# Hybrid attention/Hyena step: a free list for weight buffers, earlier splits, two more adaLN chunks on VectorE

## The chip, the cores and the metric

The kernel runs on one core of one Trainium2 chip. The time is the device time of one launch in microseconds (us), the median of the runs; lower is better. One further execution is profiled, and everything said of single instructions is read from that one.

## The reference

Two trunk layers run over 256 latent and 128 context tokens of width 2048. Cut to what matters:

```python
for l in range(2):
    mod_ctx = silu(c_ctx) @ w_ada[l] + b_ada[l]      # adaLN: 2048 -> 3*2048
    mod_lat = silu(c) @ w_ada[l] + b_ada[l]
    ctx, kv = mixer_layer(ctx, mod_ctx, None, None, ...)
    lat, _ = mixer_layer(lat, mod_lat, rope, cache[l], ...)

def mixer_layer(x, mod, ...):
    shift, scale, gate = split(mod, 3)
    h = rmsnorm(x, norm_g) * (1 + scale) + shift
    q, k, v, g_att, hy_in, g_hy = split(h @ w_in)    # hy_in is x0 | x1 | vv
    att = attend(rope(norm(q)), rope(norm(k)), v) * silu(g_att)
    x0, x1, vv = split(short_conv(hy_in))
    z = vv * x1
    y = irfft(rfft(z) * rfft(filter)) + bias * z
    hy = x0 * y * silu(g_hy)
    return x + gate * (concat(att, hy) @ w_out)
```

All is float32. Outputs are the normed trunk of both token groups and the keys and values of the context.

## The kernel before

**Layout.** The 384 tokens stand as columns, a feature block of 128 as partitions; the width 2048 is 16 such tiles. `XM` holds the trunk, later the mixed result. A float32 product is made of three fp32r ones: weights and activations are each split into a high and a low part, and hi·hh, hi·hl and lo·hh are summed. `make_h` writes the normed, modulated input as `hh` and `hl`. `split` makes `hi` of half a weight unit by a copy with a cast on ACT (L151) and `lo` by a subtraction on DVE (L152). Each has SPB = 4 buffers.

**Units.** The work is a list of units of 128x2048 weights, loaded by SP as two half buffers `raw` of 128x1024 from a ring of RAWB = 6, which main weights and adaLN weights share (`load_to`, in the order of the list). Main units are "b" (q, k, v: 12 each layer with 36 tiles of 512 columns), "a" (48 matmuls of 384 columns each; per layer 8 for x0, 16 for x1 and z in turn, 8 attention gates, 8 Hyena gates) and "o" (16 of the output projection, L774 adds gate times result to the residual tile `xo`, which L769 loads on SP). An adaLN chunk of 512 features is four units: 12 chunks a layer. The first eight chunks of layer 0 (scale, shift) are computed at the start, with the k and q units in between as the string START says. The other twelve that layer 0's main steps carry are layer 0's gate and layer 1's scale and shift; the four of layer 1's gate are done in layer 1.

**adaLN, two ways.** A chunk marked P in HOW runs on PE: four matmuls a unit (L199) with the conditioning as the stationary operand, then a copy, four transposes (L210), a reduction. A chunk marked D runs on DVE: eight multiply-adds a unit (L264 the first, L266 the rest) into two accumulators `pa`, and at the end of the chunk the column sum on PE (L282) and two transposes (L290). The DVE operations stand in a queue `vq`; `run_q` issues `u.dq` of them at the end of a main step.

**Order.** The schedule is manual: what the program issues first comes first on its engine. A main step of unit u issues, in order: what is left of u's splits, the first half's split of the next unit (if its loads have been issued), u's matmuls, the second half's split of the next unit, u's evacuation (conversion of a convolution, gate, or residual), background work up to a budget (`run_bg`: attention, filters, Hyena transforms), and `dq` adaLN operations. `plan` puts an adaLN unit between two main units and sets `dq` from the lists R_*, at most LB + 8 operations waiting. SP's loads run RAWB half buffers ahead of the unit in hand, whatever its kind.

**The seam.** The last output unit forms the sum of squares' reciprocal root (`rstd1`, `rstd2`), then layer 1's k units start with `make_h` of tiles 0 to 3, and of the others between the k units. A `make_h` of a tile is one DVE product (L347), two ACT passes with scale and bias (L350), a cast into `hh` (L352) and a DVE subtraction into `hl` (L354, L358).

Of the kernel before, what the change touches and what calls it, by code (L numbers as in the profile page):

```python
# [66 lines left out]
def step_kernel(ctx, tc, xT, vec, cst, delta, zfeat, fw, ada, wb, wc, wo, ck, cv, qk1, yT, nk, nv):  # L67
# [3 lines left out]
    rawp = pool("rawp", RAWB)  # L71
# [54 lines left out]
    state = {"load": 0, "step": 0, "dq": 0}  # L126

    class Unit:
        def __init__(self, src, kind, **kw):
            self.src, self.kind, self.kw = src, kind, kw  # L130
            self.raw, self.nxt, self.dq = [None, None], None, 0
            self.mid = False
            self.hi, self.lo = [None, None], [None, None]

    def load_to(n):
        while state["load"] < min(n, 2 * len(units)):
            i, h = divmod(state["load"], 2)
            u = units[i]
            u.raw[h] = rawp.tile([128, 1024], F32, name="raw", tag="raw")
            nc.sync.dma_start(out=u.raw[h], in_=u.src[:, h * 1024:(h + 1) * 1024])  # L140
# [3 lines left out]

    def split(u, h):
        if u is None or u.kind == "ada" or u.hi[h] is not None:
            return
        hi = hip.tile([128, 1024], F32R, name="hi", tag="hi")
# [4 lines left out]
        u.hi[h], u.lo[h] = hi, lo  # L153

# [38 lines left out]
    def ada_mm(u):  # L193
# [4 lines left out]
        for t in range(4):  # L198
            mm(part[32 * t:32 * t + 32, :], scT[:, kc * 4 + t, :], u.raw[t // 2][:, (t % 2) * 512:(t % 2 + 1) * 512],  # L199
               start=(kc == 0), stop=(kc == 3))  # L200
        if kc == 3:
# [38 lines left out]
    pacc = {}  # L240


    vq = []

    def ada_acc(u):
# [5 lines left out]
        def done():  # L251
            st["left"] -= 1
            if st["left"] == 0:
                urgent.append((state["step"] + 1, lambda: ada_sum(l, ch, st)))

        def op(t, v):
            if v not in st:
                st[v] = accs_p.tile([128, 512], F32, name=f"pa{v}", tag=f"pa{v}")
# [8 lines left out]
            done()  # L267
# [5 lines left out]
    def run_q(q, n):  # L273
        for _ in range(n):
# [66 lines left out]
    def make_h(l, kts):  # L341
        ts = []
        for kt in kts:
# [3 lines left out]
            nc.vector.tensor_tensor(t[:, :T], XM[:, kt, :], r[:, :T], ALU.mult)  # L347
        for kt, t in zip(kts, ts):
            for a, b, v in SEG:
                nc.scalar.activation(t[:, a:b], t[:, a:b], AF.Identity, bias=mod[l][:, kt, v:v + 1],  # L350
                                     scale=asc[l][:, kt, v:v + 1])
            nc.scalar.copy(hh[:, kt, :], t[:, :T])  # L352
        for kt, t in zip(kts, ts):
            nc.vector.tensor_tensor(hl[:, kt, :], t[:, :T], hh[:, kt, :].bitcast(F32), ALU.subtract)  # L354
# [437 lines left out]
    def ada_units(l, ch, n=0, how="P"):  # L792
# [276 lines left out]
```

## Time and profile before

| what | value |
|---|---|
| time before, median of 3 runs | 1563.02 us (1561.33 to 1567.05) |
| the profiled execution's own time, and its span | 1566.88 us, 1565.1 us |
| TensorE clock granted, mean | 0.982 |
| busy: PE, PEld, DVE, ACT, POOL | 1500.5, 1302.5, 951.8, 598.8, 22.4 us |
| instructions on PE, DVE, ACT | 8046, 1522, 991 |
| moved by DMA | 286.48 MB, mean 183 GB/s |

PE is busy for 96% of the span, DVE for 61%. The run is cut below at ends of main units on PE:

| stretch of the run, us | main units |
|---|---|
| 0 to 170.0 | start: adaLN of layer 0 with most of its k and q units |
| 170.0 to 195.0 | the last two of those k and q units |
| 195.0 to 283.5 | second half of q, then v, layer 0 (4 + 4 units) |
| 283.5 to 704.0 | x0, x1 and z, gates but the last, layer 0 (39) |
| 704.0 to 861.4 | last gate and output projection, layer 0 (17) |
| 861.4 to 914.3 | the seam and k, layer 1 (4) |
| 914.3 to 949.3 | first half of q, layer 1 (4) |
| 949.3 to 1019.5 | second half of q, then v, layer 1 (4 + 4) |
| 1019.5 to 1401.5 | x0, x1 and z, gates but the last, layer 1 (39) |
| 1401.5 to 1546.6 | last gate and output projection, layer 1 (17) |
| 1546.6 to 1565.1 | final norm and store |

Of adaLN work the start has eight chunks on PE. The stretch from 195.0 to 861.4 has six on PE and six on DVE, layer 1 four on DVE. A row of a view of stretches gives its start and end, its length, then the busy time and the number of instructions of PE, PEld (weight loads of TensorE), DVE, ACT and POOL, the granted clock, the share of the 16 DMA engines that was busy, and GB/s. A view restricted to one line leaves out the engines that the line does not use. A row of single instructions begins with start and length; a bracket gives the wait ahead of the first and what ended it. A row of waits ends with total, count and longest; a row of a group, after the bar, with busy time, mean in ns, then the idle time ahead of its instructions and what ended most of it.

### The profile page before, as it was taken

How to read it: one execution, taken by the hardware profiler on the slowest of the kernel's cores; microseconds unless marked ns; L12 is line 12 of the kernel's file. 1: busy time of each engine (PE TensorE's matmuls, PEld its weight loads, DVE VectorE, ACT ScalarE, POOL GpSimd, SP SyncE). 2: the span in 40 equal slices, each digit the busy share in tenths (PEclk: the TensorE clock that was granted, in tenths of full speed). 3: DMA queues.
4: the chain of work that ended last, by engine and by line, in shares of the span. 5: the costliest groups of instructions: out<-in, count | busy, mean ns of one | idle time of the engine just before them, and what ended most of it. 6: DMA issues, size and time to landing. Idle time of an engine off the chain costs nothing.

```text
span 1565.1 us, 20551 instructions
## 1 busy us (share of the span) xinstructions
PE 1500.5 (96%) x8046; PEld 1302.5 (83%) x8046; DVE 951.8 (61%) x1522; ACT 598.8 (38%) x991; POOL 22.4 (1%) x45
## 2 busy tenths in 40 slices
PE   9998989999999999998899899999999999999996
PEld 5355667878998888998899578899999999999995
DVE  5743466655576666577767464675677767675444
ACT  2433444445433233224323554455543332234331
POOL 1100000000000000000000000000000000000000
PEclk9999999999999999999999899999999999999998
DMA  9867745645566575354677134343345354464432
GB/s 352 340 242 269 268 149 180 208 162 175 179 211 234 184 235 194 138 201 156 220 241 237 65 124 139 135 155 132 124 155 208 103 182 141 165 204 151 154 126 81
DMA packets 81770, 286.48 MB, mean 183 GB/s; under 512 B 9638, under 2 KB 14056, under 8 KB 81160
## 3 DMA queue, kind: packets, MB, share of 16 engines
q1 hardware_dynamic: 78872, 276.63, 51.2%
q0 software_dynamic: 2800, 8.53, 1.4%
q8 instruction: 63, 1.03, 0.3%
q14 instruction: 35, 0.29, 0.1%
HBM read 271.49 MB, written 13.63 MB: 182 GB/s over the span
## 4 chain that ended last, share of the span: by engine, by line
PE 78%; DMA 10%; DVE 6%; ACT 5%; issue 1%; SPq 0%; DVEq 0%; ACTq 0%
PE acc L726 17%; PE acc L728 17%; PE acc L727 17%; DMA raw<-in_wc 6%; PE acc L702 5%; PE acc L701 5%; PE acc L703 5%; PE adab L199 3%; DVE lo L152 2%; ACT hi L151 2%; DMA raw<-in_wb 2%; PE bgb L423 1%; ACT tt L350 1%; PE bgb L563 1%; DVE hl L358 1%
## 5 line engine op out<-in xcount | busy, mean ns | idle before, releaser
L726 PE MATMUL acc<-hh,hi 128*128 128x384 f32 x1792 | 613.5, 342 | 5.5 <-ACT hi L151 4.2
L728 PE MATMUL acc<-hh,lo 128*128 128x384 f32 x1792 | 604.6, 337 | 11.1 <-DVE lo L152 11.1
L727 PE MATMUL acc<-hl,hi 128*128 128x384 f32 x1792 | 603.3, 337 | 1.2 <-DVE hl L358 1.0
L152 DVE TENSOR_TENSOR lo<-raw,hi 128x1024 fp32r<-128x1024 f32 x288 | 344.5, 1222 | 232.6 <-ACT hi L151 230.6
L151 ACT CAST hi<-raw 128x1024 fp32r<-128x1024 f32 x288 | 295.4, 1047 | 342.6 <-DMA raw<-in_wc 253.9
L726 PEld LDWEIGHTS acc<-hh,hi 128*128 128x128 f32 x1792 | 337.5, 188 | 29.0 <-issue 8.9
L728 PEld LDWEIGHTS acc<-hh,lo 128*128 128x128 f32 x1792 | 337.4, 188 | 15.1 <-DVE lo L152 15.0
L727 PEld LDWEIGHTS acc<-hl,hi 128*128 128x128 f32 x1792 | 337.4, 188 | 5.0 <-DVE hl L358 2.3
L266 DVE SCALAR_TENSOR_TENSOR pa<-raw,scT,pa 128x512 f32<-128x512 f32 x300 | 206.4, 746 | 0.0
L701 PE MATMUL acc<-hi,hh 128*128 128x512 f32 x384 | 160.5, 418 | 13.0 <-ACT hh L352 8.8
L702 PE MATMUL acc<-lo,hh 128*128 128x512 f32 x384 | 157.2, 409 | 4.2 <-DVE lo L152 4.2
L703 PE MATMUL acc<-hi,hl 128*128 128x512 f32 x384 | 157.1, 409 | 0.0
L701 PEld LDWEIGHTS acc<-hi,hh 128*128 128x128 f32 x384 | 75.0, 195 | 41.4 <-ACT hh L352 14.1
L702 PEld LDWEIGHTS acc<-lo,hh 128*128 128x128 f32 x384 | 75.1, 195 | 23.7 <-DVE lo L152 6.8
L309 ACT ACTIVATE tt<-XM 128x384 f32<-128x384 f32 x48 | 24.8, 524 | 175.9 <-DVE XM L774 171.6
L703 PEld LDWEIGHTS acc<-hi,hl 128*128 128x128 f32 x384 | 74.9, 195 | 20.5 <-DVE hl L354 2.7
L774 DVE SCALAR_TENSOR_TENSOR XM<-acc,mod,xo 128x256 f32<-128x256 f32 x64 | 23.8, 413 | 87.3 <-PE acc L728 62.5
L199 PE MATMUL adab<-raw,scT 128*32 128x512 f32 x448 | 63.5, 610 | 5.1 <-DMA raw<-in_ada 5.0
L350 ACT ACTIVATE tt<-tt,mod,asc 128x256 f32<-128x256 f32 x64 | 31.5, 540 | 36.4 <-DVE tt L347 36.3
L354 DVE TENSOR_TENSOR hl<-tt,hh 128x384 fp32r<-128x384 f32 x32 | 17.9, 559 | 40.8 <-ACT hh L352 40.8
L199 PEld LDWEIGHTS adab<-raw,scT 128*32 128x32 f32 x448 | 10.4, 108 | 36.7 <-issue 24.5
L620 DVE SCALAR_TENSOR_TENSOR z<-acc,V,z 128x255 f32<-128x255 f32 (+1 forms) x64 | 25.1, 414 | 20.8 <-ACT z L616 19.7
(159 smaller groups left out, 1066.3 us busy)
## 6 DMA issues: line engine op xcount, KB each, us to landing
raw<-in_ada SPq DMA_DIRECT2D x192, 512.0 KB, 4.9
raw<-in_wc SPq DMA_DIRECT2D x160, 512.0 KB, 4.8
raw<-in_wb SPq DMA_DIRECT2D x64, 512.0 KB, 5.3
raw<-in_wo SPq DMA_DIRECT2D x64, 512.0 KB, 5.3
P<-Hd SPq DMA_DIRECT2D x4, 1536.0 KB, 9.2
XM<-in_xT SPq DMA_DIRECT2D x4, 768.0 KB, 9.1
Hd<-P POOLq DMA_DIRECT2D x12, 256.0 KB, 6.1
Hd<-P SPq DMA_DIRECT2D x12, 256.0 KB, 6.6
```

What stands on the lines that cost most here:

```text
L151: nc.scalar.copy(hi, src)
L152: nc.vector.tensor_tensor(lo, src, hi.bitcast(F32), ALU.subtract)
L199: mm(part[32 * t:32 * t + 32, :], scT[:, kc * 4 + t, :], u.raw[t // 2][:, (t % 2) * 512:(t % 2 + 1) * 512], start=(kc == 0), stop=(kc == 3))
L266: nc.vector.scalar_tensor_tensor(out=acc, in0=w, scalar=sc, in1=acc, op0=ALU.mult, op1=ALU.add)
L350: nc.scalar.activation(t[:, a:b], t[:, a:b], AF.Identity, bias=mod[l][:, kt, v:v + 1], scale=asc[l][:, kt, v:v + 1])
L620: nc.vector.scalar_tensor_tensor(out=out[:, o:o + n], in0=bank[:, i:i + n], scalar=w(k), in1=out[:, o:o + n], op0=ALU.mult, op1=ALU.add)
L701: mm(accs[g][m], hh[:, kt, ms], wh[:, k, :], start=first, stop=False)
L702: mm(accs[g][m], hh[:, kt, ms], wl[:, k, :], start=False, stop=False)
L703: mm(accs[g][m], hl[:, kt, ms], wh[:, k, :], start=False, stop=last)
L726: mm(b[:, :T], wh, hh[:, kt, :], start=(kt == 0), stop=False)
L727: mm(b[:, :T], wh, hl[:, kt, :], start=False, stop=False)
L728: mm(b[:, :T], wl, hh[:, kt, :], start=False, stop=(kt == 15))
```

## The change

The ring of half buffers becomes eight named tiles in a free list. `fetch` takes one and issues its load; `release` gives it back at the point of the program where its last reader is issued: for main weights behind the split, for adaLN on PE behind the unit's matmuls, for adaLN on DVE behind the last operation on that half. `load_main` loads main weights as long as buffers are free and at most MAINB = 4 are held by main weights; `load_ada` loads an adaLN unit if two are free and at most ADAB = 4 are held. `plan` is gone: adaLN units are taken from `todo` by `load_ada` at the end of a step.

A step now also splits the first half of the unit after the next, between its evacuation and the background work, so that attention and Hyena work stands behind that split. The order of a step is: matmuls, second half's split of the next unit, loads, evacuation, first half's split of the unit after the next, loads, background work, up to PPS = 2 adaLN units on PE, `dq` adaLN operations, adaLN loads. SPB is 3 for 4.

HOW marks four of the twelve chunks of layer 0 for PE, eight for DVE (before six and six); the four in layer 1 stay on DVE. The lists R_* are new, with R_1 for layer 1. Column sums of finished chunks go through a queue `sums`, which is emptied before the accumulators are reused.

`make_h` is rewritten: per tile two DVE operations (latent and context columns) that apply reciprocal root and scale, two ACT passes that add the bias and write `hh` directly, two DVE operations that form `hl`. A tile had one DVE product, three ACT operations and one DVE subtraction.

```diff
-RAWB = 6
-SPB = 4
+RAWB = 8
+SPB = 3
-HOW = 'PPDDPDPDPDPDDDDD'
+HOW = 'PPDDDDPPDDDDDDDD'
-LB = 2
+MAINB, ADAB, PPS = 4, 4, 2
-R_O = [5] * 15 + [0]
+R_O = [4] + [6] * 14 + [5]
...
+    def fetch(u, h, of=None):
+        u.raw[h], u.of = free.pop(0), of
+        if of:
+            held[of] += 1
+        nc.sync.dma_start(out=u.raw[h], in_=u.src[:, h * 1024:(h + 1) * 1024])
+
+    def release(u, h):
+        free.append(u.raw[h])
+        if u.of:
+            held[u.of] -= 1
...
+    def load_main():
+        load_start()
+        if state["load"] == 2 * len(units):
+            while free and held["main"] < MAINB and state["main"] < 2 * len(mains):
+                i, h = divmod(state["main"], 2)
+                fetch(mains[i], h, "main")
+                state["main"] += 1
+
+    def load_ada():
+        while todo and len(free) >= 2 and held["ada"] <= ADAB - 2:
+            u = todo.pop(0)
+            for h in range(2):
+                fetch(u, h, "ada")
+            if u.kw["how"] == "P":
+                by_pe.append(u)
+            else:
+                ada_acc(u)
...
     def make_h(l, kts):
...
-            nc.vector.tensor_tensor(t[:, :T], XM[:, kt, :], r[:, :T], ALU.mult)
+            for a, b, v in SEG:
+                nc.vector.scalar_tensor_tensor(out=t[:, a:b], in0=XM[:, kt, a:b], scalar=asc[l][:, kt, v:v + 1],
+                                               in1=r[:, a:b], op0=ALU.mult, op1=ALU.mult)
         for kt, t in zip(kts, ts):
             for a, b, v in SEG:
-                nc.scalar.activation(t[:, a:b], t[:, a:b], AF.Identity, bias=mod[l][:, kt, v:v + 1],
-                                     scale=asc[l][:, kt, v:v + 1])
-            nc.scalar.copy(hh[:, kt, :], t[:, :T])
+                nc.scalar.activation(hh[:, kt, a:b], t[:, a:b], AF.Identity, bias=mod[l][:, kt, v:v + 1])
         for kt, t in zip(kts, ts):
-            nc.vector.tensor_tensor(hl[:, kt, :], t[:, :T], hh[:, kt, :].bitcast(F32), ALU.subtract)
+            for a, b, v in SEG:
+                nc.vector.scalar_tensor_tensor(out=hl[:, kt, a:b], in0=t[:, a:b], scalar=mod[l][:, kt, v:v + 1],
+                                               in1=hh[:, kt, a:b].bitcast(F32), op0=ALU.add, op1=ALU.subtract)
...
             {"b": b_evac, "a": a_evac, "o": o_evac}[u.kind](u)
...
-            run_bg(EB if startup else 2.5)
+            if startup:
+                run_bg(EB)
+                continue
+            if u.nxt is not None:
+                split(u.nxt.nxt, 0)
+            load_main()
+            run_bg(2.5)
+            for a in by_pe[:PPS]:
+                ada_mm(by_pe.pop(0))
             run_q(vq, u.dq)
+            load_ada()
```

The rows below are the program's order on one engine. Names are the program's: `raw` or `raw_1xx` a half buffer, `pa` an adaLN accumulator, `xo` a residual tile, `lo` the low part of a weight half, `x2` two alike in a row.

SP's loads in the output projection of layer 0, about two steps of before:

```order
L140 DMA raw<-in_ada 128x1024 x2
L769 DMA xo<-in_xT 128x384
L140 DMA raw<-in_wo 128x1024 x2
L769 DMA xo<-in_xT 128x384
L140 DMA raw<-in_wo 128x1024 x2
```

and of the changed kernel, from one residual load to three later:

```order
L141 DMA raw_105<-in_ada 128x1024
L141 DMA raw_103<-in_ada 128x1024
L817 DMA xo<-in_xT 128x384
L141 DMA raw_107<-in_wo 128x1024
L141 DMA raw_108<-in_wo 128x1024
L141 DMA raw_109<-in_ada 128x1024
L141 DMA raw_104<-in_ada 128x1024
L817 DMA xo<-in_xT 128x384
L141 DMA raw_110<-in_wo 128x1024
L141 DMA raw_106<-in_wo 128x1024
L817 DMA xo<-in_xT 128x384
```

Before, an adaLN unit's loads stood ahead of every second residual load; now they stand ahead of three in four.

DVE in an output unit of layer 0, from one residual sum (two pieces, L774, later L822) to the next, before:

```order
L774 SCALAR_TENSOR_TENSOR XM<-acc,mod_97,xo 128x256
L774 SCALAR_TENSOR_TENSOR XM<-acc,mod_97,xo 128x128
L313 TENSOR_TENSOR acc_93<-acc_93,tt 128x384
L266 SCALAR_TENSOR_TENSOR pa_5527<-raw,scT,pa_5527 128x512
L266 SCALAR_TENSOR_TENSOR pa_5525<-raw,scT,pa_5525 128x512
L266 SCALAR_TENSOR_TENSOR pa_5527<-raw,scT,pa_5527 128x512
L152 TENSOR_TENSOR lo<-raw,hi 128x1024 x2
L774 SCALAR_TENSOR_TENSOR XM<-acc,mod_97,xo 128x256
```

and in the changed kernel:

```order
L822 SCALAR_TENSOR_TENSOR XM<-acc,mod_94,xo 128x256
L822 SCALAR_TENSOR_TENSOR XM<-acc,mod_94,xo 128x128
L359 TENSOR_TENSOR acc_90<-acc_90,tt 128x384
L185 TENSOR_TENSOR lo<-raw_108,hi 128x1024
L312 SCALAR_TENSOR_TENSOR pa_5558<-raw_103,scT,pa_5558 128x512
L312 SCALAR_TENSOR_TENSOR pa_5560<-raw_103,scT,pa_5560 128x512
L312 SCALAR_TENSOR_TENSOR pa_5558<-raw_109,scT,pa_5558 128x512
L312 SCALAR_TENSOR_TENSOR pa_5560<-raw_109,scT,pa_5560 128x512
L312 SCALAR_TENSOR_TENSOR pa_5558<-raw_109,scT,pa_5558 128x512
L312 SCALAR_TENSOR_TENSOR pa_5560<-raw_109,scT,pa_5560 128x512
L185 TENSOR_TENSOR lo<-raw_110,hi 128x1024
L822 SCALAR_TENSOR_TENSOR XM<-acc,mod_94,xo 128x256
```

One of the two lo moved ahead of the adaLN operations, of which there are six instead of three to five. In this step the second operation is the last on half buffer raw_103.

DVE in a step with attention work, between the conversion of a convolution and the next one, before (L532 and L535 are the softmax):

```order
L532 TENSOR_REDUCE mx<-bgb 128x1
L535 RECIPROCAL z<-z 128x1
L532 TENSOR_REDUCE mx<-bgb 128x1
L535 RECIPROCAL z<-z 128x1
L266 SCALAR_TENSOR_TENSOR pa_2409<-raw,scT,pa_2409 128x512
L266 SCALAR_TENSOR_TENSOR pa_2407<-raw,scT,pa_2407 128x512
L266 SCALAR_TENSOR_TENSOR pa_2409<-raw,scT,pa_2409 128x512
L152 TENSOR_TENSOR lo<-raw,hi 128x1024 x2
```

and in the changed kernel (L580 and L583 are the softmax):

```order
L185 TENSOR_TENSOR lo<-raw_104,hi 128x1024
L580 TENSOR_REDUCE mx<-bgb 128x1
L583 RECIPROCAL z<-z 128x1
L580 TENSOR_REDUCE mx<-bgb 128x1
L583 RECIPROCAL z<-z 128x1
L312 SCALAR_TENSOR_TENSOR pa_2137<-raw_109,scT,pa_2137 128x512
L312 SCALAR_TENSOR_TENSOR pa_2139<-raw_109,scT,pa_2139 128x512
L312 SCALAR_TENSOR_TENSOR pa_2137<-raw_109,scT,pa_2137 128x512
L312 SCALAR_TENSOR_TENSOR pa_2139<-raw_109,scT,pa_2139 128x512
L312 SCALAR_TENSOR_TENSOR pa_2137<-raw_103,scT,pa_2137 128x512
L312 SCALAR_TENSOR_TENSOR pa_2139<-raw_103,scT,pa_2139 128x512
L185 TENSOR_TENSOR lo<-raw_107,hi 128x1024
```

One lo moved ahead of the softmax, and six adaLN operations stand where three stood. At the seam the order on DVE behind the reciprocal root is now a lo, five adaLN operations, then the first `make_h`; before it was that `make_h` at once.

More of the change, by code (lines that the diff above doesn't have):

```diff
@@ L125, in step_kernel @@
     units = []
-    state = {"load": 0, "step": 0, "dq": 0}
+    state = {"load": 0, "step": 0, "main": 0}
+    held = {"main": 0, "ada": 0}
+    free = [one.tile([128, 1024], F32, name=f"raw{n}") for n in range(RAWB)]
     class Unit:
@@ L131, in __init__, with load_start @@
             self.raw, self.nxt, self.dq = [None, None], None, 0
-            self.mid = False
+            self.mid, self.of = False, None
             self.hi, self.lo = [None, None], [None, None]
-    def load_to(n):
-        while state["load"] < min(n, 2 * len(units)):
+    def fetch(u, h, of=None):
[7 more added lines that the diff above has]
+            held[u.of] -= 1
+    def load_start():
+        while state["load"] < 2 * len(units) and free:
             i, h = divmod(state["load"], 2)
-            u = units[i]
-            u.raw[h] = rawp.tile([128, 1024], F32, name="raw", tag="raw")
-            nc.sync.dma_start(out=u.raw[h], in_=u.src[:, h * 1024:(h + 1) * 1024])
+            fetch(units[i], h)
             if h == 1 and 4 <= i < 8:
@@ L153, in split @@
         u.hi[h], u.lo[h] = hi, lo
+        release(u, h)
     bg = []
@@ L200, in ada_mm @@
                start=(kc == 0), stop=(kc == 3))
+        for h in range(2):
+            release(u, h)
         if kc == 3:
@@ L238, in have_rstd, with run_sums @@
             ready(j)
-    pacc = {}
-    vq = []
+    pacc, sums = {}, []
+    def run_sums():
+        while sums:
+            sums.pop(0)()
+    vq, by_pe = [], []
     def ada_acc(u):
@@ L249, in ada_acc, with done @@
         st = pacc[0]
-        def done():
+        left = [4, 4]
+        def done(h):
             st["left"] -= 1
+            left[h] -= 1
+            if left[h] == 0:
+                release(u, h)
             if st["left"] == 0:
-                urgent.append((state["step"] + 1, lambda: ada_sum(l, ch, st)))
+                sums.append(lambda: ada_sum(l, ch, st))
+                urgent.append((state["step"] + 1, run_sums))
         def op(t, v):
             if v not in st:
+                run_sums()
                 st[v] = accs_p.tile([128, 512], F32, name=f"pa{v}", tag=f"pa{v}")
@@ L273, in run_q @@
     def run_q(q, n):
-        for _ in range(n):
+        for _ in range(min(n, len(q))):
             q.pop(0)()
@@ L860, in start @@
         nc.sync.dma_start(out=V, in_=vec)
-        load_to(2)
+        for h in range(2):
+            fetch(units[0], h)
+        state["load"] = 2
         nc.scalar.activation(scT[:, :, 0:2], V[:, V_C:V_C + 32].rearrange("p (k v) -> p k v", v=2), AF.Silu)
@@ L951, in step_kernel @@
             split(u, 1)
-            near = u.nxt is not None and u.nxt.raw[1] is not None
+            near = u.nxt is not None and (not startup or u.nxt.raw[1] is not None)
             if near:
```

63 lines of the change are left out of this document (25 added, 38 removed).

## The prediction

> **What bounds it now.** I read the stretches of the run first, then the waits, then single steps. The two layers do the same matrix work, so I cut both at the same units of it. The rows give length, busy time (and instructions) of PE, PEld, DVE, ACT and POOL, the granted clock, the DMA share and GB/s:
>
> ```profile
> 0.00:170.00 170.00, 159.33 (x689) 82.35 (x690) 81.18 (x143) 61.20 (x100) 8.85 (x20) 0.97 0.81 300
> 195.00:283.50 88.50, 81.03 (x362) 60.89 (x361) 53.78 (x87) 37.98 (x78) 1.63 (x3) 0.96 0.50 172
> 949.30:1019.50 70.20, 70.20 (x318) 56.75 (x317) 42.42 (x66) 34.59 (x65) 1.09 (x2) 1.00 0.40 135
> 283.50:704.00 420.50, 412.28 (x2392) 372.88 (x2390) 262.77 (x428) 151.72 (x247) 0.54 (x1) 1.00 0.56 192
> 1019.50:1401.50 382.00, 382.00 (x2208) 367.96 (x2207) 263.00 (x417) 146.69 (x238) 0.54 (x1) 1.00 0.45 155
> 704.00:861.40 157.40, 147.99 (x846) 143.41 (x845) 110.37 (x167) 52.27 (x73) 8.14 (x15) 0.99 0.64 213
> 1401.50:1546.60 145.10, 143.49 (x827) 141.61 (x827) 68.47 (x101) 47.63 (x68) 0.00 (x0) 1.00 0.38 129
> 861.40:914.30 52.90, 44.05 (x161) 30.38 (x160) 27.86 (x46) 33.23 (x61) 1.08 (x2) 0.87 0.20 68
> 1430.00:1513.00 83.00, 83.00 (x480) 83.00 (x480) 36.66 (x50) 25.67 (x32) 0.00 (x0) 1.00 0.46 155
> ```
>
> They are: start; second half of q with v, layer 0 and 1; x0 up to the last gate unit, 0 and 1; that gate unit with the output projection, 0 and 1; the seam between the layers; ten dense output units. The last row gives the yardstick: 480 matmuls in 83.0 us, 8.3 us for a unit of 48. TensorE bounds layer 1. Layer 0 is longer by 18.3, 38.5 and 12.3 us. Part of that is adaLN work on PE, the rest is stalls:
>
> ```profile
> PE acc L728 <- DVE lo L152: 10.5, 11, 3.3
> ACT hi L151 <- DMA raw<-in_wc: 205.2, 66, 9.3
> SPq L140 <- DVE pa L266: 195.0, 48, 10.6
> 283.50:704.00 420.50, 21.31 (x160) 3.15 (x160) 1.00 0.56 192
> L210 PE MATMUL bgb<-C,tt 128*128 128x128 f32 x56 | 9.3, 291 | 0.7 <-ACT tt L203 0.7
> L282 PE MATMUL bgb<-pa,ones 128*32 128x256 f32 x80 | 6.9, 391 | 1.0 <-DVE pa L266 1.0
> L290 PE MATMUL bgb<-C,tt 128*128 128x128 f32 x20 | 4.1, 289 | 0.5 <-ACT tt L284 0.5
> ```
>
> The first three are waits between 170 and 870 us, with total, count and longest; the fourth is L199 alone, adaLN on PE: 160 records, 20 units, 1.07 us each. The chain reads backwards: PE waits for lo, lo for hi, hi for a weight load, and SP holds that load because the ring's next buffer is still read by an adaLN step on DVE.
>
> By the Trainium skill, Perfetto Trace Analysis, "Identifying the Most-Contended Engine", matmul busy time misjudges headroom and LDWEIGHTS busy time is the measure. The trace agrees: in the long stretch PE shows 8.2 us idle, PEld 47.6; by the first alone the stalls there would be capped near 8 us and the sum would come out some 5 us later.
>
> **Fewer chunks on PE.** Two chunks go to DVE. Each gives back 4 units of 1.07 us and its transposes (14 chunks share the 9.3 us of L210, 0.66 each), 4.9 us; each adds column sums (10 chunks share 6.9 + 4.1), 1.1 us. In all −7.6 us of PE. By place: the long stretch keeps 8 of its 20 PE units, the one before it gets 8 instead of 4. On DVE two chunks are 64 operations, priced next.
>
> **Splits earlier.** In an attention step DVE now does, in order, the conversion of a convolution, lo of the second unit ahead, the softmax, six adaLN operations, and the other lo. Rows of before (start, length; then ACT's first pass of a convolution, four steps of layer 1, the cast of a weight half):
>
> ```profile
> 364.36 1.64 DVE L620 SCALAR_TENSOR_TENSOR XM<-acc,V,XM 128x255 f32<-128x255 f32 x4
> 365.92 0.55 DVE L532 TENSOR_REDUCE mx<-bgb 128x1 f32<-128x384 f32 x1
> 368.69 2.06 DVE L266 SCALAR_TENSOR_TENSOR pa<-raw,scT,pa 128x512 f32<-128x512 f32 x3
> 741.02 3.40 DVE L266 SCALAR_TENSOR_TENSOR pa<-raw,scT,pa 128x512 f32<-128x512 f32 x5
> 744.34 2.35 DVE L152 TENSOR_TENSOR lo<-raw,hi 128x1024 fp32r<-128x1024 f32 x2
> L616 ACT ACTIVATE XM<-acc,V 128x384 f32<-128x384 f32 x16 | 10.7, 670 | 27.7 <-PE acc L728 27.7
> 1047.80:1094.10 46.30, 46.30 (x257) 43.37 (x257) 28.64 (x52) 24.87 (x48) 0.00 (x0) 1.00 0.39 128
> L151 ACT CAST hi<-raw 128x1024 fp32r<-128x1024 f32 x288 | 295.4, 1047 | 342.6 <-DMA raw<-in_wc 253.9
> ```
>
> Convolution 1.56 (to the next start), softmax 2.77 (365.92 to 368.69, its waits for ACT inside), an adaLN operation 0.66 apart (five in 3.40, from 741.02 to the lo at 744.34), a lo 1.14 apart (two in 2.35). With 0.75 for ACT's pass ahead (0.67 and the way) that is 0.75 + 1.56 + 1.14 + 2.77 + 6 × 0.66 + 1.14 = 11.3 us. The four steps of layer 1 take PE 46.3, 11.6 each: DVE just fits. It may also run late: lo of the second half is first wanted half a unit, 4.1 us, into the next unit but one. So the x0 and x1 steps should not stall on lo. Nor on loads:
>
> ```profile
> raw<-in_wc SPq DMA_DIRECT2D x160, 512.0 KB, 4.8
> P<-Hd SPq DMA_DIRECT2D x4, 1536.0 KB, 9.2
> ```
>
> With four main half buffers of its own account, a half is fetched when the half two units ahead of it has been split, some 16 us before it is wanted; it lands in 4.8 and may well wait behind an adaLN load on SP. The filter spectra, the other transfer on SP here, are issued two steps ahead of their use and land in 9.2. The long stretch becomes 382.0 + 8 × 1.07 + 1.3 + 1.1 + 1 left = 394, **−26** us (−13 if the stalls stay, −28 if all go).
>
> The stretch before it gets those 4.9 us of PE work. Its stalls, 88.5 − 70.2 − 4.9 = about 13, could fall by as much, since its first two steps no longer have adaLN operations, or stay, since an extra lo now stands ahead of the q/k norms. I take a fall by the same 4.9, in all **0** (−8 to +5).
>
> **Output projection of layer 0.** Here the change hurts. Its residual load xo stands on SP behind the adaLN loads, and these now wait for operations of the step before. What that does is already in the profile, on a light step of before with three adaLN operations:
>
> ```profile
> 778.56 2.07 DVE L266 SCALAR_TENSOR_TENSOR pa<-raw,scT,pa 128x512 f32<-128x512 f32 x3
> 781.04 0.42 SPq L769 DMA_DIRECT2D xo<-in_xT  x1
> 786.72 0.48 DVE L774 SCALAR_TENSOR_TENSOR XM<-acc,mod,xo 128x256 f32<-128x256 f32 x1 [3.82 <-DMA xo<-in_xT]
> DMA to landing us min/median/max: 4.2/5.1/6.5
> 1463.82 0.74 DVE L774 SCALAR_TENSOR_TENSOR XM<-acc,mod,xo 128x256 f32<-128x256 f32 x2 [3.67 <-PE acc L728]
> 1466.10 2.36 DVE L152 TENSOR_TENSOR lo<-raw,hi 128x1024 fp32r<-128x1024 f32 x2 [0.38 <-ACT hi L151]
> ```
>
> The adaLN operations end at 780.63, xo is issued 0.41 later, and DVE stands idle 3.82 us for it. From 755 us on xo lands 5.1 us after issue (4.2 to 6.5): 5.5 from the release. Before, only every second xo follows such a load and the lighter steps make it up. Afterwards nearly every one does. A step is then XM to lo 2.28 (the two 146x rows), lo 1.14, six operations 3.96, lo 1.14: 8.5 us. Between the operation that frees the load and the next XM stand, by the order's rows, 3.8 us (after the second operation), 2.5 (fourth), 1.1 (sixth), or 5.1 (none), in turn. So four steps take 4 × 8.5 − 12.5 + 4 × 5.5 = 43.5 us on DVE against PE's 33.8 with one column sum. Over 15 steps that is 36 us, less 3 for the first, which is still on time: 33 over the 145.1 that layer 1 needs, so 178 or 179 for 157.4, **+22** us. Landings of 4.2 and 6.5 move it by 15 times the difference: +8 and +43.
>
> A rule speaks the other way. By the Trainium skill, DMA: Bandwidth & Descriptors, "Latency and other measured facts", a DMA's fixed cost is about 2 us. With that, plus 0.4, only the 1.1 case would wait and this term would be near −10; the trace's 4.2 to 6.5 for 192 KB disagrees, so the sum goes by the trace.
>
> **Seam.** After rstd DVE now does a lo, which waits for ACT's copy and cast, and five adaLN operations before the first make_h:
>
> ```profile
> 864.96 0.56 DVE L329 TENSOR_TENSOR tt<-C,r 128x384 f32<-128x384 f32 x1
> 867.32 0.48 ACT L338 COPY acc<-bgb 128x384 f32<-128x384 f32 x1 [2.61 <-PE bgb L337]
> 867.90 0.55 DVE L347 TENSOR_TENSOR tt<-XM,bgb 128x384 f32<-128x384 f32 x1
> 869.49 0.51 ACT L352 CAST hh<-tt 128x384 fp32r<-128x384 f32 x1
> 878.86 1.02 DVE L347 TENSOR_TENSOR tt<-XM,acc 128x384 f32<-128x384 f32 x2
> 884.54 1.02 DVE L347 TENSOR_TENSOR tt<-XM,acc 128x384 f32<-128x384 f32 x2
> ```
>
> ACT's copy ends at 867.80. A cast of a weight half, 1.05, + 1.14 for lo + 5 × 0.66 puts the first make_h at 873.3, 5.4 us after 867.90. PE and its clock (0.87 in this stretch) wait with it. But a round of two make_h tiles took 5.68 us (878.86 to 884.54), with DVE waiting for ACT; the change takes one cast of 0.51 a tile off ACT, and DVE's two extra operations a tile run while it would wait. Five rounds of 4.7 give back 5. I take **0** (−4 to +5).
>
> **Start.** Loads run one unit further ahead, eight half buffers for six:
>
> ```profile
> PE adab L199 <- DMA raw<-in_ada: 5.0, 4, 2.2
> ```
>
> PE waits 5.0 us for adaLN loads, all here, and the mean clock of 0.97 over 170 us costs as much again. A unit more, 1.05 MB, is 3.5 us at this stretch's 300 GB/s, more than the longest wait; I take half of both, **−5** (−10 to +1). The smaller hi/lo pool, 3 for 4, delays a second half until half a unit has been used, covered by the 4.1 us above. Layer 1 and the tail: **0**, PE has no stall to lose there.
>
> **Sum.** −5 + 0 − 26 + 22 + 0 = −9. The profiled run has span 1565.1 and took 1566.88, 3.9 above the median of 1563.02; the difference goes on the median. That is 1554.
>
> **Rivals.** (1) *xo is hidden*: the landing shortens as the queue ahead of it empties. Then the output units take about 147, −10 for +22, and the total is 1522. For it: DVE never waited for xo in layer 1. Against: there no adaLN load stands ahead of it. Chance 0.17. (2) *The head start does nothing*: DVE, at 11.3 of 11.6 us, falls behind and the long stretch keeps its 13 us; 1567. For it: the narrow fit; against: the 4.1 us of slack. 0.13. (3) *Slower*: the output projection's xo lands late. It decides from a mean landing of about 6.3 us, where 15 × 1.2 = 18 us more come on top; at 6.5 it gives 1575. For it: 6.5 in the range and more loads on the queue; against: the median of 5.1. 0.15. (4) *The forecast*, 1542 to 1563: 0.55.
>
> Below 0.5% a measurement of this kernel can hardly be told from no change. Of the forecast 0.30 lies under 1555, 0.23 within the bound, 0.02 above. Rival 1 is all faster, rival 2 mostly same (0.02, 0.10, 0.01), rival 3 mostly slower (0, 0.02, 0.13). Faster 0.49, same 0.35, slower 0.16. The range, 1523 to 1575, reaches to the ends of rivals 1 and 3 and leaves a tenth at each side.
>
> **What would show it.** Right: the stretch from x0 to the last gate near 394 us; DVE XM waiting for xo some 3 us in most output units of layer 0, that stretch near 178; the waits of SP for adaLN operations gone from the x0 steps' main loads; PE's idle time before the first k unit of layer 1 up by 5 us. Wrong: xo waits of under 1 us, or lo waits on PE in the x0 steps.

## The result

The changed kernel takes 1601.87 us (median of 4 runs, 1599.10 to 1605.41) against 1562.17 us for the kernel before (4 runs): the ratio is 1.0251, 95% interval 1.0219 to 1.0284. It is slower by about 40 us, where the prediction had 9 us faster; the time lies outside the range of 1523 to 1575.

### The profile page after: what moved, and what is told of

It reads as the page before. It is cut to its first block, busy times and chain, and to the rows that moved or that the text cites. A ratio compares the mean times of both kernels' runs of the same rounds, so it can differ in the third digit from the quotient of the medians.

```text
span 1597.3 us, 20568 instructions
## 1 busy us (share of the span) xinstructions
PE 1495.8 (94%) x7994; PEld 1311.6 (82%) x7994; DVE 1007.2 (63%) x1650; ACT 577.6 (36%) x959; POOL 22.4 (1%) x45
## 4 chain that ended last, share of the span: by engine, by line
PE 45%; DVE 4%; DMA 2%; ACT 1%; issue 1%; SPq 0%; DVEq 0%; ACTq 0%
PE acc L774 11%; PE acc L775 11%; PE acc L776 11%; PE acc L749 3%; PE acc L750 2%; PE acc L751 2%; DVE pa L312 2%; DMA xo<-in_xT 2%; DVE lo L185 1%; ACT hi L184 1%; PE bgb L611 1%; PE bgb L594 1%; PE bgb L328 1%; DVE XM L833 1%; PE bgb L702 0%
## 5 line engine op out<-in xcount | busy, mean ns | idle before, releaser
L774 PE MATMUL acc<-hh,hi 128*128 128x384 f32 x1792 | 617.9, 345 | 0.9 <-ACT hi L184 0.9
L185 DVE TENSOR_TENSOR lo<-raw,hi 128x1024 fp32r<-128x1024 f32 x288 | 351.2, 1221 | 249.2 <-ACT hi L184 248.0
L184 ACT CAST hi<-raw 128x1024 fp32r<-128x1024 f32 x288 | 299.5, 1044 | 325.5 <-PE acc L775 216.0
L774 PEld LDWEIGHTS acc<-hh,hi 128*128 128x128 f32 x1792 | 340.2, 190 | 18.2 <-issue 11.8
L312 DVE SCALAR_TENSOR_TENSOR pa<-raw,scT,pa 128x512 f32<-128x512 f32 x360 | 246.6, 744 | 0.0
L822 DVE SCALAR_TENSOR_TENSOR XM<-acc,mod,xo 128x256 f32<-128x256 f32 x64 | 23.8, 413 | 67.4 <-PE acc L776 37.9
L328 PE MATMUL bgb<-pa,ones 128*32 128x256 f32 x96 | 16.6, 531 | 46.9 <-DVE pa L312 46.9
L233 PE MATMUL adab<-raw,scT 128*32 128x512 f32 x384 | 54.0, 604 | 3.2 <-DMA raw<-in_ada 3.2
L328 PEld LDWEIGHTS bgb<-pa,ones 128*32 128x32 f32 x96 | 3.8, 126 | 54.4 <-DVE pa L312 27.2
L668 DVE SCALAR_TENSOR_TENSOR z<-acc,V,z 128x255 f32<-128x255 f32 (+1 forms) x64 | 25.2, 414 | 31.4 <-ACT z L664 30.2
L668 DVE SCALAR_TENSOR_TENSOR XM<-acc,V,XM 128x255 f32<-128x255 f32 (+1 forms) x64 | 25.2, 414 | 24.6 <-ACT XM L664 23.5
## 6 DMA issues: line engine op xcount, KB each, us to landing
XM<-in_xT SPq DMA_DIRECT2D x4, 768.0 KB, 11.6
```

The lines of the kernel that those rows point to most:

```text
L184: nc.scalar.copy(hi, src)
L185: nc.vector.tensor_tensor(lo, src, hi.bitcast(F32), ALU.subtract)
L312: nc.vector.scalar_tensor_tensor(out=acc, in0=w, scalar=sc, in1=acc, op0=ALU.mult, op1=ALU.add)
L328: mm(b[o:o + 32, 0:256], ones[:, 0:32], acc[v][:, h * 256:(h + 1) * 256], start=True, stop=True)
L668: nc.vector.scalar_tensor_tensor(out=out[:, o:o + n], in0=bank[:, i:i + n], scalar=w(k), in1=out[:, o:o + n], op0=ALU.mult, op1=ALU.add)
L774: mm(b[:, :T], wh, hh[:, kt, :], start=(kt == 0), stop=False)
```

## The profile after

The profiled execution took 1599.1 us, its span is 1597.3 us. It is cut at the ends of the same main units as before: the start with the last k and q units, second half of q with v, x0 up to the last gate, that gate with the output projection, the seam with k, and layer 1 from q on. The columns are those of the stretches before.

```profile
0.00:185.90 185.90, 176.23 (x774) 97.94 (x774) 100.88 (x197) 66.18 (x112) 8.86 (x20) 0.96 0.85 318
185.90:276.00 90.10, 84.85 (x402) 61.91 (x401) 54.19 (x90) 41.35 (x82) 1.64 (x3) 0.98 0.64 218
276.00:694.90 418.90, 401.92 (x2299) 374.62 (x2298) 297.24 (x478) 148.20 (x242) 0.54 (x1) 0.98 0.51 177
694.90:877.50 182.60, 154.45 (x848) 146.57 (x847) 122.56 (x189) 49.55 (x71) 8.12 (x15) 0.93 0.57 193
877.50:935.60 58.10, 40.56 (x161) 31.63 (x160) 42.16 (x89) 23.69 (x47) 1.08 (x2) 0.79 0.33 114
935.60:1579.40 643.80, 634.95 (x3505) 597.05 (x3504) 380.15 (x588) 247.38 (x403) 2.18 (x4) 0.99 0.40 138
```

| stretch | before | after | predicted difference | measured |
|---|---|---|---|---|
| start, last k and q | 195.0 | 185.9 | −5 | −9.1 |
| second half of q, v | 88.5 | 90.1 | 0 | +1.6 |
| x0 to the last gate, layer 0 | 420.5 | 418.9 | −26 | −1.6 |
| output projection, layer 0 | 157.4 | 182.6 | +22 | +25.2 |
| seam and k | 52.9 | 58.1 | 0 | +5.2 |
| layer 1 from q on (before: 914.3 to 1546.6) | 632.3 | 643.8 | 0 | +11.5 |

With 0.6 less in the tail the measured column sums to the spans' difference, 32.2 us. The long stretch kept PE's idle time: 418.90 − 401.92 = 17.0 us, against 8.2 before; 15.0 of the 17.0 are now spent in front of column sums. In layer 1, where almost nothing was to change, 11.5 us are new.

One group of the page, the column sums of the DVE chunks, and three waits of the whole run (total, count, longest):

```profile
L328 PE MATMUL bgb<-pa,ones 128*32 128x256 f32 x96 | 16.6, 531 | 46.9 <-DVE pa L312 46.9
```

```profile
PE bgb L328 <- DVE pa L312: 46.9, 9, 11.5
DVE XM L822 <- DMA xo<-in_xT: 29.4, 12, 5.3
PE acc L776 <- DVE lo L185: 4.1, 7, 0.7
```

The column sum was the harmless row of the profile before: 1.0 us of idle time ahead of it in the whole run. Now PE stands 46.9 us in front of it. The waits for lo, which the change was expected to remove, did fall, from 11.1 us on the page of before to 4.1.

One such wait, in an attention step of layer 1, on PE and then on DVE (start, length, count at the end, idle time ahead and its releaser in brackets):

```profile
1123.27 0.62 PE L328 MATMUL bgb<-pa,ones 128*32 128x256 f32 x4
1127.10 1.07 PE L328 MATMUL bgb<-pa,ones 128*32 128x256 f32 x4 [3.20 <-DVE pa L312]
1128.10 0.69 PE L774 MATMUL acc<-hh,hi 128*128 128x384 f32 x1
```

```profile
1120.84 1.64 DVE L668 SCALAR_TENSOR_TENSOR XM<-acc,V,XM 128x255 f32<-128x255 f32 x4 [2.25 <-ACT XM L664]
1122.40 1.22 DVE L185 TENSOR_TENSOR lo<-raw,hi 128x1024 fp32r<-128x1024 f32 x1
1123.53 0.55 DVE L580 TENSOR_REDUCE mx<-bgb 128x1 f32<-128x384 f32 x1
...
1126.23 0.16 DVE L583 RECIPROCAL z<-z 128x1 f32<-128x1 f32 x1 [0.79 <-ACT P L582]
1126.31 0.73 DVE L312 SCALAR_TENSOR_TENSOR pa<-raw,scT,pa 128x512 f32<-128x512 f32 x1
1126.96 0.48 DVE L310 TENSOR_SCALAR pa<-raw,scT 128x512 f32<-128x512 f32 x1
```

At this step the `vq` queue holds the last operation of one chunk (the L312 at 1126.31) and the first ones of the next (L310). In front of the next chunk's first operation the program calls `run_sums`, so the column sum is issued in the same step, behind this step's matmuls on PE. PE has nothing left ahead of it and stands until DVE has done the evacuation, a lo, the softmax and the last adaLN operation; the matmuls of the next unit, whose operands are ready, stand behind the sum. Before, `plan` never let a step mix two chunks, and the sum came a whole step later. By the Trainium skill, PSUM — Partial Sum Buffer, section "Engine vs sequencer instructions", matmuls start and complete in program order; the trace agrees: no matmul of L774 starts ahead of the sum that waits until 1127.10.

The output projection is late in the main for the reason that the prediction gave: DVE waits 27.6 us for xo there. PE also stands 23.1 us in front of three column sums in this stretch, which the prediction did not have. DVE, from one residual sum to the next but one:

```profile
715.33 0.74 DVE L822 SCALAR_TENSOR_TENSOR XM<-acc,mod,xo 128x256 f32<-128x256 f32 x2 [2.61 <-DMA xo<-in_xT]
...
723.05 0.74 DVE L822 SCALAR_TENSOR_TENSOR XM<-acc,mod,xo 128x256 f32<-128x256 f32 x2 [0.44 <-DMA xo<-in_xT]
724.38 0.56 DVE L359 TENSOR_TENSOR acc<-acc,tt 128x384 f32<-128x384 f32 x1 [0.59 <-ACT tt L355]
725.31 1.23 DVE L185 TENSOR_TENSOR lo<-raw,hi 128x1024 fp32r<-128x1024 f32 x1 [0.38 <-ACT hi L184]
726.46 1.41 DVE L312 SCALAR_TENSOR_TENSOR pa<-raw,scT,pa 128x512 f32<-128x512 f32 x2
728.37 0.49 DVE L310 TENSOR_SCALAR pa<-raw,scT 128x512 f32<-128x512 f32 x1 [0.51 <-PE bgb L328]
```

DVE waits for xo in 11 of these units, and here too a chunk ends in the step (L312, then L310 behind the sum). At the seam, on DVE:

```profile
885.85 0.74 DVE L822 SCALAR_TENSOR_TENSOR XM<-acc,mod,xo 128x256 f32<-128x256 f32 x2 [1.87 <-DMA xo<-in_xT]
...
893.86 1.23 DVE L185 TENSOR_TENSOR lo<-raw,hi 128x1024 fp32r<-128x1024 f32 x1 [3.26 <-ACT hi L184]
895.00 3.40 DVE L312 SCALAR_TENSOR_TENSOR pa<-raw,scT,pa 128x512 f32<-128x512 f32 x5
898.31 0.73 DVE L394 SCALAR_TENSOR_TENSOR tt<-XM,asc,bgb 128x256 f32<-128x256 f32 x2
```

The last residual sum starts at 885.85, 8.4 us after PE finished the last output unit at 877.5: the lag that DVE has gathered is paid here. ACT's copy of the root ended at 892.88, and the first make_h starts 5.4 us later, as priced.

## The experiments

Times are medians, ratios those to the kernel before on the same chip, with the 95% interval; the kernel before took 1562.2 to 1563.3 us in each set of runs, so medians of different sets are compared directly. Three theories stood at first: **S**, the column sum issued in its own step; **X**, the late residual load; and against S, **D**, that DVE has no slack in those steps and PE would only wait elsewhere.

### Chunk and column sum kept a step apart

The entries of the queue carry a mark, `q[0][0]`, for a chunk's first operations.

```diff
     def run_q(q, n):
-        for _ in range(min(n, len(q))):
-            q.pop(0)()
+        more = min(state["carry"], 2) if n else 0
+        n, state["carry"] = n + more, state["carry"] - more
+        while n and q:
+            if q[0][0] and sums:
+                state["carry"] += n
+                break
+            n -= 1
+            q.pop(0)[1]()
```

> The changed kernel, but a step's adaLN operations stop at the end of a chunk until that chunk's column sum has been issued behind the next unit's matmuls; the operations left over are carried on, at most two more a step. Theory S (the column sum): a sum issued in the same step as the chunk's last DVE operations makes PE stand until DVE has worked through that step. Then the waits of the column sum for DVE fall from 46.9 us to under 5, the stretch from x0 to the last gate of layer 0 falls from 418.9 to 394 us (390 to 400), v to the last gate of layer 1 loses about 13 us, the output projection with the seam at most 5, and the time is about 1562 us (1554 to 1570). Rival D (DVE is full): in those steps DVE has no slack, PE then waits for lo where it waited at the sum; the long stretch of layer 0 stays above 410 and the time above 1585.

Measured: 1558.68 us, ratio 0.9972 (0.9958 to 0.9987), 43 us under the changed kernel.

```profile
275.90:675.30 399.40, 397.33 (x2299) 372.14 (x2298) 296.73 (x478) 147.90 (x242) 0.54 (x1) 1.00 0.55 185
675.30:853.20 177.90, 157.08 (x848) 149.41 (x847) 122.79 (x190) 49.84 (x72) 8.09 (x15) 0.94 0.59 199
```

```profile
PE bgb L336 <- DVE pa L314: 8.0, 2, 5.0
DVE XM L833 <- DMA xo<-in_xT: 37.3, 12, 5.1
```

S holds and D falls. The same DVE work is in the long stretch (296.7 us) and PE idles 2 us there instead of 17; layer 1 from the second half of q to the last gate takes 453.6 us instead of 467.4. The two sums that still wait, 8.0 us where under 5 were expected, lie in the output projection. That stretch stays long, 177.9 us, so with the residual load late its price is for the most part not the sum's.

### The residual load a step earlier

```diff
-            if u.kind == "o":
+            if u.kind == "o" and u.kw["f"] == 0:
                 load_xo(u)
...
             load_main()
+            if u.nxt is not None and u.kind == "o" and u.nxt.kind == "o":
+                load_xo(u.nxt)
             run_bg(2.5)
```

> The changed kernel, but the residual load of an output unit is issued one step earlier, ahead of the adaLN loads of the step before. Theory X (DVE sets the pace of layer 0's output projection, and its waits for xo are part of that pace): the 29.4 us that DVE waits for xo go, output projection and seam of layer 0 fall together from 240.7 us (182.6 + 58.1) by 20 to 27, the rest stays, time about 1578 us (1572 to 1584). Rival S alone (there too only the column sums cost PE time, and DVE would have caught up between them): the waits for xo go, but output projection and seam fall by under 8 us and the time stays above 1592.

Measured: 1573.88 us, ratio 1.0071 (1.0048 to 1.0093), 28 us under the changed kernel.

```profile
693.60:856.50 162.90, 149.19 (x848) 144.56 (x847) 127.06 (x196) 51.69 (x72) 8.11 (x15) 0.96 0.67 220
856.50:907.30 50.80, 40.15 (x160) 31.36 (x159) 37.23 (x83) 22.53 (x45) 1.08 (x2) 0.83 0.34 114
```

Output projection and seam lose 27.0 us together, and DVE's waits for xo there fall to 4.3 us. X holds.

### Both

> Both edits: chunk boundaries kept apart from their column sums, and the residual load a step earlier. If the two costs lie in different places they add: long stretch of layer 0 near 394, output projection and seam near 215, time about 1538 us (1530 to 1548), 1.5% under the kernel before. If both are one lag of DVE that is paid at whichever wait comes first, the second edit adds under 8 us to the better of the two single ones.

Measured: 1520.70 us, ratio 0.9724 (0.9704 to 0.9744). The output projection:

```profile
673.40:821.20 147.80, 146.01 (x848) 142.67 (x847) 125.17 (x194) 50.91 (x72) 8.10 (x15) 1.00 0.74 240
```

The two gains, 43 and 28 us, add, and 10 us more come, so the kernel is faster than the range expected: with xo early the output projection takes 162.9 us, with the sums apart 177.9, with both 147.8. Each of the two waits hides part of the other there.

### Both, and a clear seam

```diff
-R_O = [4] + [6] * 14 + [5]
+R_O = [4] + [6] * 14 + [0]
...
-            if u.nxt is not None:
+            if u.nxt is not None and (u.kind != "o" or u.kw["f"] < 15):
                 split(u.nxt.nxt, 0)
```

> Both edits, and in the last output unit of layer 0 no split of the unit after the next and no adaLN operations ahead of the first make_h. The prediction priced these at 5.4 us on the path to the first make_h (a cast 1.05, lo 1.14, five operations 3.3): by that the seam is about 5 us shorter than with both edits alone, time near 1533 us. Rival: the split that is left out is only done later, in front of k's second unit, and PE waits for it there; then the gain is under 2 us.

Measured: 1516.55 us, ratio 0.9696 (0.9675 to 0.9717). The interval overlaps that of the kernel with both edits, so the time alone does not settle it. The stretch of seam and k went from 51.6 to 44.4 us while the output projection before it grew by 2.6: 4.6 us in all, near the 5.4 priced and above the rival's 2.

### The early split taken out

```diff
-            if u.nxt is not None and (u.kind != "o" or u.kw["f"] < 15):
-                split(u.nxt.nxt, 0)
```

This is on the base of the last kernel: the same split is then done at the start of the next step, behind the background work and the adaLN operations instead of ahead of them.

> As the kernel with both edits and the clear seam (1516.6 us), but without the split of the first half two units ahead: that split is done in front of the next unit's matmuls, as in the kernel before. Theory H (the head start removes the waits for lo that the kernel before has in layer 0): about 13 us of stalls come back, most in the stretch from x0 to the last gate of layer 0 (398 to 405 or more), time about 1528 us (1523 to 1536). Rival L (the loads running ahead from the free list did it, the split's place does nothing): within 3 us of 1516.6.

Measured: 1505.02 us, ratio 0.9630 (0.9607 to 0.9653). Both theories missed: without the early split the kernel is 11.5 us faster. PE's waits, and the two stretches of layer 0:

```profile
PE acc L760 <- DVE lo L185: 4.0, 3, 2.5
PE bgb L522 <- DVE P L555: 1.6, 1, 1.6
```

```profile
270.60:666.10 395.50, 395.24 (x2300) 370.95 (x2299) 295.07 (x476) 149.42 (x242) 0.54 (x1) 1.00 0.55 187
666.10:810.80 144.70, 144.67 (x847) 142.26 (x846) 126.76 (x197) 51.63 (x72) 8.09 (x15) 1.00 0.76 249
```

PE is idle for 0.3 us in 540 us, without the head start. With it PE waited 5.3 us for the norms' products (L522) and 3.1 us for the column sums. PE's waits for lo grew only from 1.5 to 4.0 us, so lo was nearly always in time from the later place. DVE's waits for xo in the output projection, 7.5 us with the head start, are gone. Between the two profiled runs the output projection takes 5.7 us less, the long stretch 2.6 and the seam 1.5. Another 2.7 us lie in the start, where the edit changes nothing, so a few us of the 11.5 may be noise.

### The early split taken out of the changed kernel

The same edit on the changed kernel alone, with column sums and residual load as they are there.

> The changed kernel without the early split, nothing else (the split of the first half two units ahead goes back in front of the next unit's matmuls). Where DVE is late in the order, the early lo stands ahead of what PE waits for: softmax, adaLN operations of the column sum, residual sum. Theory H' (the early split delays those by a lo and its wait for ACT, some 2 us, at each of the twelve column sums): the waits of the column sum fall from 46.9 to about 25 us and the time from 1602 to about 1577 us (1567 to 1587). Rival (it costs what it costs without these waits): 11.5 us, time about 1590 us.

Measured: 1555.21 us, ratio 0.9953 (0.9936 to 0.9969), 47 us under the changed kernel.

```profile
PE bgb L330 <- DVE pa L314: 23.1, 8, 5.5
DVE XM L827 <- DMA xo<-in_xT: 14.5, 8, 4.3
```

The wait of the sums came out as forecast (25 expected, 23.1), the time did not (1577 expected): the waits for xo halved too, from 29.4 us. The likely reason, argued from the order and not tested by itself, is that the operation that frees an adaLN buffer, and with it the load ahead of xo on SP, comes earlier on DVE. The output projection went from 182.6 to 165.1 us. One line that puts a lo ahead feeds both costs.

### Six chunks on PE again

On the base of 1516.55 us, with `HOW = 'PPDDPDPDPDPDDDDD'`.

> The same base, with the marks of before: six of layer 0's twelve chunks on PE and six on DVE instead of four and eight. The prediction priced the two chunks at 7.6 us of PE in all: by that the time is 1524 us (1521 to 1528). Rival (what PE saves DVE pays, since DVE sets the pace in places): DVE's 64 fewer operations give back as much, within 3 us of 1516.6.

Measured: 1530.81 us, ratio 0.9793 (0.9771 to 0.9815), 14.3 us slower than its base. The direction is as priced, the size is nearly twice the 7.6 us.

```profile
274.30:685.00 410.70, 406.03 (x2357) 372.86 (x2356) 283.95 (x457) 148.41 (x243) 0.55 (x1) 1.00 0.57 193
```

The stretch from x0 on grew from 398.1 to 410.7 us, of which 10.3 is busy PE (395.8 on the base). The page's busy time of the PE chunks grew from 55.1 to 65.3 us, 1.28 us a unit instead of the 1.07 taken. The seam added 3.3 us, for which no cause was sought.

### The old make_h

On the same base, make_h as before.

> The same base, with make_h as before (one DVE product, three ACT operations, one DVE subtraction a tile). The prediction priced the new form at 5 us in the k units of layer 1: by that the seam with k grows from 44.4 to about 49 us, the start by 0 to 3, time about 1522 us (1520 to 1526). Rival (PE's matmuls hide it): the seam grows by under 2 us, time within 2 us of 1516.6.

Measured: 1527.80 us, ratio 0.9774 (0.9751 to 0.9798), 11.3 us slower than its base.

```profile
820.60:875.80 55.20, 43.95 (x159) 30.04 (x158) 29.99 (x47) 33.24 (x61) 1.08 (x2) 0.88 0.27 93
```

The seam with k takes 10.8 us more, not 5. The gain of the new form lies there: all other stretches together are 2.8 us shorter than on the base, and the profiled spans differ by 8.0 us.

### The kernel before with mixed chunks

```diff
-                while u.dq < room[i - 8 * l] and queue and queue[0] == cur:
+                while u.dq < room[i - 8 * l] and queue:
...
             if v not in st:
+                run_sums()
```

> The kernel before, with one thing added: a step may hold the last adaLN operations of one chunk and the first of the next, and the column sum is then issued between them, in that step. By the program's order this happens at four of the ten chunk ends, two in each layer. Theory S: PE stands at these four sums until DVE has worked through the step, 3 to 6 us each; layer 1, which had no such waits, grows by about 9 us, and the time goes to about 1577 us (1570 to 1585). Rival F (only with the free list, the early split and the shorter buffer pool does the sum come to hurt): the waits of the sum stay under 3 us in all, and the time within 5 us of 1563.

Measured: 1575.35 us, ratio 1.0085 (1.0058 to 1.0111), 12.5 us slower than the kernel before.

```profile
L288 PE MATMUL bgb<-pa,ones 128*32 128x256 f32 x80 | 9.3, 415 | 17.1 <-DVE pa L272 17.1
1021.40:1409.60 388.20, 383.65 (x2208) 368.28 (x2207) 264.58 (x419) 146.31 (x238) 0.55 (x1) 1.00 0.46 154
```

The mechanism works without free list, early split or the smaller hi/lo pool: 17.1 us of waits at four sums, 15.3 us more in layer 0's long stretch and 6.2 in layer 1's, where 9 were expected. Layer 0's output projection became 10.2 us shorter; some adaLN work moved out of it (DVE is busy there for 105.5 us, before 110.4), but no run shows that this is the whole cause.

### The kernel before with the early residual load

The same edit of `load_xo` as above, on the kernel before.

> The kernel before with the residual load of an output unit issued one step earlier and nothing else. Theory X at half dose: there every second residual load stands behind adaLN loads; layer 0's output projection (157.4 us, 145.1 in layer 1) loses about 9 us and the time goes to about 1554 us (1549 to 1558). Rival: DVE's lighter steps make it up anyway and PE's idle time there has another cause; then the time stays above 1560.

Measured: 1558.18 us, ratio 0.9970 (0.9957 to 0.9983). The output projection of layer 0 takes 152.2 us for 157.4: 5.2 less instead of 9, and the time just misses the expected range. X shows here too, but small: DVE's waits for xo fell from 24.8 to 4.7 us, so most of them had cost PE nothing, presumably because DVE's lighter steps made them up.

### Main loads behind the adaLN loads

```diff
                 split(u.nxt, 1)
-            load_main()
+            if startup:
+                load_main()
...
-            load_main()
             if u.nxt is not None and u.kind == "o" and u.nxt.kind == "o":
                 load_xo(u.nxt)
```

> The fastest kernel so far (both edits, no adaLN operations in the last output unit, no early split; 1505.0 us), but main weights are loaded only at the top of a step, so on SP behind the adaLN loads of the step before, which wait for DVE. Theory L (the gain in layer 0's long stretch comes from main loads that no longer stand behind adaLN loads): PE waits for hi and lo again, the stretch from x0 to the last gate grows from 395.5 to about 408 us, time about 1520 us (1513 to 1530). Rival P (it comes from fewer units on PE and from the split adaLN buffers alone, and a load a step late still lands in time): under 4 us slower.

Measured: 1500.62 us, ratio 0.9607 (0.9587 to 0.9626): not slower than its base, and the lowest time of all. It is 4.4 us under the base, but the two intervals overlap, so a gain is not shown. The long stretch:

```profile
267.90:662.00 394.10, 394.10 (x2299) 370.80 (x2298) 295.18 (x476) 149.44 (x242) 0.55 (x1) 1.00 0.56 188
```

Theory L falls: with a main load a whole step ahead of its split, it may stand behind the adaLN loads.

### The kernel before with eight half buffers

```diff
-RAWB = 6
-SPB = 4
+RAWB = 8
+SPB = 3
```

> The kernel before with eight half buffers in its ring and three hi/lo buffers (before six and four), nothing else. Theory B (the stalls of layer 0's long stretch come from a ring that runs too short ahead; two more half buffers do what the free list does): the stretch from x0 to the last gate falls from 420.5 to about 410 us, the start by about 7, time about 1547 us (1540 to 1553). Rival A (a load for PE still stands behind a buffer that an adaLN step on DVE holds, however long the ring; the separate accounts are needed): the long stretch stays within 4 us and the time above 1555.

Measured: 1533.71 us, ratio 0.9824 (0.9797 to 0.9851): two constants make it 29 us faster, more than expected. The long stretch of layer 0, and between 170 and 870 us ACT's waits for main loads, which were 205.2 us before:

```profile
269.80:678.40 408.60, 408.60 (x2391) 373.06 (x2390) 262.57 (x426) 151.47 (x243) 0.54 (x1) 1.00 0.57 196
```

```profile
ACT hi L151 <- DMA raw<-in_wc: 11.0, 8, 3.8
```

Theory B holds: PE is busy for the whole stretch, and what is left over layer 1's 382.0 us is adaLN work on PE. The old stalls came from a ring that ran too short ahead; separate accounts are not needed for them. The long stretch became 11.9 us shorter although PE showed only 8.2 us of idle time in it. More than was expected came from ahead of x0: that part is 13.7 us shorter, the output projection 4.3.

## Why the prediction was wrong

**Fewer chunks on PE, the step that failed most.** It read "each adds column sums (10 chunks share 6.9 + 4.1), 1.1 us". That is the sum's work, taken from rows in which it hardly waited (1.0 us in all). The sum's place in the order was not looked at: `run_sums` in `op` issues it in the step of its last operands. It cost 46.9 us of waits, in the long stretch, the output projection and layer 1; the kernel before waits as well once its steps may mix chunks. With it apart, the long stretch fell to 399.4 us and layer 1 to its old length. The prediction asked what waits for lo, for loads and for xo, but of the waits that the new order adds it left this one out, and the 0 for layer 1 ("PE has no stall to lose there") looked only at stalls that could go. The move of the two chunks by itself, with the sums apart, is worth 14.3 us, nearly twice the 7.6 of the sum.

**Splits earlier.** The arithmetic of 11.3 of 11.6 us said that DVE just fits, and lo was nearly always in time (4.1 us of waits). But the gain was put down to the wrong thing, and what stands behind the moved lo was priced at nothing. The 394 forecast for the long stretch is met within 1.5 us by the kernel without the early split (395.5). The head start costs some 11.5 us where the sums and xo are dealt with and 47 us in the changed kernel, where PE's waits at the sums and DVE's waits for xo halve without it. What removed the old stalls is the two more half buffers: they alone, in the kernel before, take the long stretch from 420.5 to 408.6 us, with PE busy throughout; the twelve PE units fewer there, at 1.07 to 1.28 us each, give the other 13 us to 395.5. Main loads ahead of adaLN loads are not needed (394.1 with them behind).

**Output projection, +22.** The mechanism was right: the early load takes the output projection from 177.9 to 147.8 us when the sums are apart. That the +25.2 measured is so near is in part luck, since it also holds waits at column sums that were not in the price; with the sums apart the term is +20.5 (177.9 for 157.4). What was missed is that DVE leaves the stretch late. The sum was of DVE's steps, but its end was compared with PE's; the rest of the lag, 8.4 us, was paid at the seam. By the Trainium skill, DMA: Bandwidth & Descriptors, section "Latency and other measured facts", a DMA's fixed cost is about 2 us. That is no price for the whole load here: xo landed 3.7 to 6.0 us after issue, median 4.8, in the output projection of the changed kernel:

```profile
DMA to landing us min/median/max: 3.7/4.8/6.0
```

**Seam, 0.** Two terms, one right and one mis-sized. The 5.4 us ahead of the first make_h were measured as 5.4. The gain of make_h was put at 5, from rounds of two tiles in 4.7 us; it is 10.8. On DVE, in the kernel with the clear seam, two rounds start at:

```profile
837.76 1.40 DVE L404 SCALAR_TENSOR_TENSOR tt<-XM,asc,acc 128x256 f32<-128x256 f32 x4
...
841.89 1.40 DVE L404 SCALAR_TENSOR_TENSOR tt<-XM,asc,acc 128x256 f32<-128x256 f32 x4
```

A round takes 4.13 us against 5.68 before, so five give 8, and behind 831.3, where the first k unit starts, PE's four k units run without a gap. The third term, DVE's lag, was left out. 5.4 − 10.8 + 8.4 makes +3.0 of the +5.2 measured; the rest stays open.

**Start, −5.** Right: the start itself went from 170.0 to 163.5 us, −6.5. The last k and q units, which the prediction did not price, gave another 2.6.

**The rivals.** The one that ended slower was the late xo landing. The landing was not late, so the case that came true, a new wait of PE on DVE at the column sum, was not among them. The second rival held that the head start brings nothing; the runs without it bear that out, though not its reason: DVE did not fall behind with lo.

## What to carry to other kernels

When work is moved between in-order engines, find for each product the place at which the other engine asks for it: an instruction is harmless in the profile only at the distance it has there, and one that is asked for in the step of its producer stops all that stands behind it. A head start for something that was in time delays everything else on its engine; first see what waits last. When loads share a queue with loads that wait for buffers, put those that are asked for soon ahead of the others, as the residual load here; the main loads, issued a whole step ahead, did not need it.

## What the hardware showed

A wait of PE of over 3 us cost more than its length here. After the wait of 6.69 us that ended at 727.26 the granted clock was about halved for nearly 4 us; the stretches are a unit without a wait, then the time after the wait:

```profile
711.90:720.20 8.30, 8.30 (x49) 8.30 (x49) 4.52 (x8) 2.41 (x3) 0.54 (x1) 1.00 0.50 180
727.20:729.00 1.80, 1.74 (x9) 0.47 (x9) 1.15 (x3) 0.00 (x0) 0.00 (x0) 0.50 0.72 218
729.00:731.00 2.00, 2.00 (x7) 2.00 (x8) 1.81 (x3) 0.37 (x1) 0.00 (x0) 0.55 0.93 343
731.00:733.00 2.00, 2.00 (x13) 2.00 (x12) 0.00 (x0) 0.00 (x0) 0.00 (x0) 1.00 0.75 233
```

The clock is 0.50, then 0.55, then 1.00 again from 731: 1.8 × 0.5 + 2.0 × 0.45 = 1.8 us of lost work on top of the wait, by estimate. In layer 1 a matmul of L774 took 0.69 us right after a wait of only 3.20 us, where it takes 0.34 otherwise. Of the nine waits at the column sum, the eight of 3.20 to 11.48 us were followed by a clock of 0.50 to 0.54; after the ninth, of 2.31 us to 1036.11, it stayed at 1.00. By the Trainium skill, TensorE: Matmul & The Clock Gate, section "Why this matters for your kernels", gaps of PE over about 3 us between bursts are to be avoided, since the clock drops; the trace agrees, with no drop after 2.31 us and one after 3.20. A second thing: PE's busy time did not show the loss. It went from 1500.5 to 1495.8 us, with the kernel 40 us slower; the waits in front of the column sum showed it.
